# A gated-linear-attention mixer: decay factors from a running sum along the tokens, in place of matrix products with 0/1 masks

## The chip, the cores and the metric

The kernel runs on one core of a Trainium2 chip, in one launch. The metric is the device time of that launch in microseconds (us); lower is better. The engines are named as in the profile: PE multiplies matrices (PEld loads its weights), DVE does elementwise work on 128 lanes, ACT does elementwise functions and copies, POOL and SP here mostly issue transfers.

## The reference, cut to what matters

Two residual layers over 256 tokens of width 2048. Layer 0 mixes tokens with a gated recurrence (HGRN, eight heads) and an attention (FoX, eight heads); layer 1 mixes them with gated linear attention (GLA, four heads, key width 256, value width 512). Each layer ends with a feed-forward network. Float32 throughout. The part that the change touches is the GLA mixer:

```python
def gla_mixer(h, w_in, w_gate_up, b_gate, out_gain, w_out):
    q, k, v, g, g_low = jnp.split(h @ w_in, cuts, axis=-1)
    log_alpha = jax.nn.log_sigmoid(g_low @ w_gate_up + b_gate) / 16.0
    o = chunk_gated_linear_recurrence(split_heads(q, 4) * (256 ** -0.5), split_heads(k, 4),
                                      split_heads(v, 4), split_heads(log_alpha, 4))
    o = merge_heads(rms_norm(o, out_gain)) * jax.nn.silu(g)
    return o @ w_out
# recurrence: S_t = diag(exp(log_g_t)) S_{t-1} + k_t v_t^T ;  o_t = S_t^T q_t
# so score(t, s) = sum_d q[t,d] k[s,d] exp(cum[t,d] - cum[s,d]), cum = running sum of log_g, for s <= t
```

## The kernel before

**The stream.** Almost all the work is products of the 256-token activations with weights from memory, cut into *pieces* of 256 rows by 512 columns of weights. Each piece comes as float32 and is split in two: `hi`, a rounded copy made by ACT (line 166), and `lo`, the rest, made by DVE (line 168). PE then does 12 matmuls of 512 columns for it (lines 189 to 191: hi by hi, lo by hi, hi by lo; two token tiles of 128, two blocks of rows). `hi` and `lo` have four buffers each (`HIS = 4`), so the casts of piece n can start when PE has finished piece n - 4. Pieces are numbered through the program; the GLA mixer's products are pieces 392 to 487 (24 for each of four *units* C0 to C3, one for each head: part 0 gives q and k, part 1 v, part 2 the output gate), and the output projection O1 begins at piece 488.

**The recurrence of a unit** is woven between the pieces as a *job*: a list of steps to be issued within a number of pieces (`TICKS`). A scheduler then sets each engine's order from its own timeline model. For one GLA unit:

- `gla_gates`: z = low-rank gate input times `gate_up`, tokens on the partitions (line 824); log-sigmoid of z on ACT and DVE (lines 292 to 294, 827); split into a high and a low part, `lf` (lines 831 and 832).
- `Recurrence.transpose`: q and k turned so that channels lie on the partitions, `qkTs` (lines 433 to 436).
- `Recurrence.decays` (lines 448 to 456), for each token tile t and each half i of the head's channels: four matmuls `ex` of 512 columns multiply `lf` with the constant 0/1 matrix `lvl`, which sums the logs between two tokens for seven halving levels (64, 32, ... 1) and the tile's start or end; ACT takes exp of both halves from PSUM (line 455). The result `dec` has eight blocks of 128 columns.
- `Recurrence.factors`: DVE multiplies `dec` by the turned k into `kd` and by the turned q in place (line 465).
- `scores`, `cross`, `pick`, `output`: PE makes compact scores `sc` for each level (line 490), `cx` between the tiles (line 496); ACT and DVE scatter them into `st` (lines 514, 518); PE multiplies by v into `po` (lines 529 to 532).
- `gla_output`: norm, gate, turn back (`oT`, line 920), scale and split into `ct_m` (lines 375, 376), which is the operand of O1.

The layer-0 recurrence uses the same class with the same mask products.

Also on DVE, once in four pieces: the adaLN sums `mod` (line 108), a 2048-column product-and-sum.

Of the kernel before, what the change touches and what calls it, by code (L numbers as in the profile page):

```python
# [15 lines left out]
P = 128  # L16
# [13 lines left out]
# pieces of the products within which the mixers' steps are to be issued  # L30
# [9 lines left out]
# columns of the packed per-partition parameters  # L40
# [10 lines left out]
class Job:  # L51
    """Steps of arithmetic to be issued between the pieces of the streamed products, before a given piece."""
# [13 lines left out]
def build(tc, ctx, a, out):  # L66
# [212 lines left out]
    def rsqrt(dst, ss, n, width, name):  # L279
        """(ss / n + eps) ** -0.5 with one Newton step."""  # L280
# [50 lines left out]
    def norm_tile(t):  # L331
        """Normalize, modulate, transpose and split one token tile of x."""
# [47 lines left out]
    def gate_line(l, part):  # L380
        """The gate as a line in DRAM."""
# [35 lines left out]
    class Recurrence:  # L417
        """Both token tiles of one head. q, k: [P, tile, d]; lf: [P, tile, 2, d] (split); v: [P, tile, dv]."""

        def __init__(self, pool, q, k, lf, nd, name):  # L420
            self.pool, self.q, self.k, self.lf, self.nd, self.name = pool, q, k, lf, nd, name
            self.qkT, self.dec, self.kd, self.dg = {}, {}, {}, {}
            self.kc = {}
            self.s_t = st[Recurrence.count % 2]
            Recurrence.count += 1
# [31 lines left out]

        def factors(self, t, i):
# [8 lines left out]
            if t == 0:  # L467
# [6 lines left out]
                else:  # L474
                    self.kc[i] = kd[:, 0, :]
            else:
# [5 lines left out]
        def scores(self, t, levels, dst):  # L482
            """dst(n) -> PSUM [P, 64] of level n"""
            for n in levels:
                b = LEVELS[n]
                p = POS[t][b]
# [5 lines left out]
        def cross(self, diagonal):  # L492
            """Scores between the token tiles, and with diagonal those of each token with itself."""
            cx = ps_mix(f"cx_{self.name}")
            for i in range(self.nd):
                nc.tensor.matmul(cx[:, :P], self.kc[i], self.dec[1, i][:, 3, :], start=(i == 0), stop=(i == self.nd - 1))
# [10 lines left out]
        def pick(self, n, ts, src):  # L507
            """scatter the compact scores of level n; src: [P, len(ts), 64]"""
# [62 lines left out]
    def hgrn_scores(u, h):  # L571
# [3 lines left out]
        def s0():  # L575
            r = Recurrence(env["pool"], e["qg"][:, :, h * P:(h + 1) * P], e["k"][:, :, h * P:(h + 1) * P],
                           e["lf"][:, :, :, h * P:(h + 1) * P], 1, f"A{u}{h}")
# [64 lines left out]
    def fox_gates():  # L642
        """-log f, split, [token, head] per token tile; and -F in columns."""
# [157 lines left out]
    # =========================== layer 1 mixer ===========================  # L801
    def gla_low():
        """The low-rank gate input, transposed: 16 rows by w's high part, 16 by its low part, then ones for the bias."""
# [9 lines left out]
    def gla_gates(u):  # L813
        pool = env["pool"]
        f = pool.tile([P, 2, 2, 256], F32R, tag="lf", name=f"lf_C{u}", bufs=1)
        env.setdefault(("C", u), {})["lf"] = f
        c = {}

        def s0():
            gup = pool.tile([64, 256], F32, tag="gup", name=f"gup_{u}", bufs=1)  # L820
            nc.sync.dma_start(out=gup, in_=a["gate_up"][:, u * 256:(u + 1) * 256])
            z = ps_mix(f"z_C{u}").rearrange("p (t c) -> p t c", t=2)
            for t in range(2):
                nc.tensor.matmul(z[:, t], env["glT"][:, t * P:(t + 1) * P], gup, start=True, stop=True)
            sp = pool.tile([P, 2, 256], F32, tag="gt", name=f"sp_C{u}")
# [4 lines left out]
        def s1():  # L830
            nc.vector.tensor_scalar(f[:, :, 0], c["sp"], 1.0 / 16.0, None, ALU.mult)
            nc.vector.scalar_tensor_tensor(f[:, :, 1], c["sp"], 1.0 / 16.0, f[:, :, 0], ALU.mult, ALU.subtract)
# [18 lines left out]
    def gla_scores(u):  # L851
# [3 lines left out]
        def s0():  # L855
            r = Recurrence(env["pool"], e["qk"][:, :, :256], e["qk"][:, :, 256:], e["lf"], 2, f"C{u}")
            e["r"] = c["r"] = r
            if u < 2:
                nc.gpsimd.memset(r.s_t, 0.0)  # no diagonal of the HGRN units
# [4 lines left out]
        def tile_steps(t):  # L864
            def d0():
                c["r"].decays(t, 0)

            def d1():
                c["r"].decays(t, 1)
# [17 lines left out]
    def gla_output(u):  # L887
        """(steps that need v, steps that need the gate too)"""
# [217 lines left out]
    def begin_out(l, src):  # L1106
        """The old x and the gate row take buffers that the mixer's activations leave."""
# [97 lines left out]
    def begin_gla():  # L1205
        env["act"] = env["next_act"]
        open_pool("mix_b")

# [74 lines left out]
def _tiles(w, groups):  # L1283
    """w (K, N) and lists of 512 columns -> (chunk, quad, 128, 4 * 512)."""
# [70 lines left out]
```

## Time and profile before

| | us |
|---|---|
| median of three runs (lowest, highest) | 2520.81 (2519.14, 2520.96) |
| span of the profiled execution, first to last instruction | 2515.9 |
| around the span, median less span | 4.9 |
| PE busy in the span | 2450.4 (97%) |
| DVE busy | 1771.8 (70%) |
| ACT busy | 1160.2 (46%) |
| granted TensorE clock, mean share of full speed | 0.998 |

The three runs lie within 1.8 us. The GLA mixer takes the stretch from 1348 to 1681 us of the span. PE's busy time counts overlapping matmuls once, so 97% says that PE almost never stands still, not how well it is used.

### The profile page before, as it was taken

To read this page: it belongs to the slowest core of one execution; us is meant where nothing else is said; L and a number is where in the kernel's file an instruction comes from. 1 tells how busy PE (TensorE), PEld (TensorE's weight loads), DVE (VectorE), ACT (ScalarE), POOL (GpSimd) and SP (SyncE) were. 2 spreads that over 40 slices of the span, in tenths; PEclk is the share of its full clock that TensorE was granted. 3 is DMA by queue.
4 is the path that set the end of the run, shared out by engine and by line. 5 is a ranking of instruction groups with operands and counts; after the bars stand their busy time and mean duration, and the time that the engine had idled before them with its cause. 6 is when DMAs were issued, how large, how long until landed. Compare 5 with 4: busy or idle time off the path is not lost.

```text
span 2515.9 us, 28838 instructions
## 1 busy us (share of the span) xinstructions
PE 2450.4 (97%) x11316; PEld 2025.2 (80%) x11316; DVE 1771.8 (70%) x1975; ACT 1160.2 (46%) x1600; POOL 89.4 (4%) x174
## 2 busy tenths in 40 slices
PE   5899999999999999999999999999999999999999
PEld 3678887887888888888888888888788888888887
DVE  6986887877688767766777777777676545554555
ACT  4365555545434444344345545554544344344443
POOL 0000000000000000000000000000000000000000
PEclk9999999999999999999999999999999999999999
DMA  9973767885899878777776566677477555555554
GB/s 379 422 272 140 274 257 292 340 319 216 287 349 357 317 281 293 287 277 293 287 277 226 202 243 233 242 256 283 169 296 254 191 194 184 196 188 186 199 185 149
DMA packets 93850, 647.49 MB, mean 257 GB/s; under 512 B 10417, under 2 KB 10993, under 8 KB 16401
## 3 DMA queue, kind: packets, MB, share of 16 engines
q1 hardware_dynamic: 70290, 476.59, 52.1%
q0 software_dynamic: 23424, 169.07, 18.1%
q8 instruction: 88, 1.44, 0.2%
q14 instruction: 48, 0.39, 0.0%
HBM read 641.39 MB, written 4.23 MB: 257 GB/s over the span
## 4 chain that ended last, share of the span: by engine, by line
PE 92%; DVE 6%; ACT 1%; issue 0%; DMA 0%; SPq 0%; ACTq 0%; DVEq 0%
PE acc_F L191 13%; PE acc_F L190 13%; PE acc_F L189 13%; PE acc_G L189 6%; PE acc_G L191 6%; PE acc_G L190 6%; PE acc_C L191 4%; PE acc_C L189 4%; PE acc_C L190 3%; DVE mod_s L108 3%; PE acc_B L189 2%; PE acc_B L190 2%; PE acc_B L191 2%; PE acc_O L189 2%; PE acc_O L191 2%; PE acc_O L190 2%
## 5 line engine op out<-in xcount | busy, mean ns | idle before, releaser
L168 DVE TENSOR_TENSOR lo<-raw_F,hi 128x1024 fp32r<-128x1024 f32 x352 | 429.4, 1224 | 296.9 <-ACT hi L166 296.8
L166 ACT CAST hi<-raw_F 128x1024 fp32r<-128x1024 f32 x352 | 370.5, 1053 | 478.3 <-PE acc_F L191 430.0
L191 PE MATMUL acc_F<-hi,hT_f 128*128 128x512 f32 x1408 | 551.3, 392 | 1.4 <-DVE hT_f L355 1.4
L189 PE MATMUL acc_F<-hi,hT_f 128*128 128x512 f32 x1408 | 548.4, 390 | 1.8 <-ACT hT_f L354 1.8
L190 PE MATMUL acc_F<-lo,hT_f 128*128 128x512 f32 x1408 | 548.5, 390 | 0.0
L108 DVE SCALAR_TENSOR_TENSOR mod<-mod,silu_c 128x2048 f32<-128x2048 f32 x160 | 365.4, 2285 | 11.1 <-DMA mod<-in_mod_w_dram 11.1
L168 DVE TENSOR_TENSOR lo<-raw_G,hi 128x1024 fp32r<-128x1024 f32 x176 | 214.2, 1222 | 138.3 <-ACT hi L166 138.1
L191 PEld LDWEIGHTS acc_F<-hi,hT_f 128*128 128x128 f32 x1408 | 264.4, 188 | 56.6 <-DVE hT_f L355 3.0
L189 PEld LDWEIGHTS acc_F<-hi,hT_f 128*128 128x128 f32 x1408 | 264.5, 188 | 56.1 <-ACT hT_f L354 2.2
L166 ACT CAST hi<-raw_G 128x1024 fp32r<-128x1024 f32 x176 | 185.4, 1054 | 268.6 <-PE acc_G L191 224.8
L190 PEld LDWEIGHTS acc_F<-lo,hT_f 128*128 128x128 f32 x1408 | 264.3, 188 | 55.2
L189 PE MATMUL acc_G<-hi,ct_f 128*128 128x512 f32 x704 | 273.5, 389 | 1.6 <-DVE res_G L403 1.6
L191 PE MATMUL acc_G<-hi,ct_f 128*128 128x512 f32 x704 | 274.4, 390 | 0.0
L190 PE MATMUL acc_G<-lo,ct_f 128*128 128x512 f32 x704 | 273.8, 389 | 0.0
L168 DVE TENSOR_TENSOR lo<-raw_C,hi 128x1024 fp32r<-128x1024 f32 x96 | 116.8, 1222 | 58.4 <-ACT hi L166 58.0
L189 PEld LDWEIGHTS acc_G<-hi,ct_f 128*128 128x128 f32 x704 | 132.2, 188 | 29.6 <-DVE res_G L403 2.4
L189 PE MATMUL acc_C<-hi,hT_n 128*128 128x512 f32 x384 | 154.3, 402 | 0.9 <-ACT hT_n L354 0.9
L190 PEld LDWEIGHTS acc_G<-lo,ct_f 128*128 128x128 f32 x704 | 132.2, 188 | 27.4
L191 PEld LDWEIGHTS acc_G<-hi,ct_f 128*128 128x128 f32 x704 | 132.2, 188 | 27.2
L191 PE MATMUL acc_C<-hi,hT_n 128*128 128x512 f32 x384 | 150.5, 392 | 0.7 <-DVE hT_n L355 0.7
L190 PE MATMUL acc_C<-lo,hT_n 128*128 128x512 f32 x384 | 150.9, 393 | 0.0
L166 ACT CAST hi<-raw_C 128x1024 fp32r<-128x1024 f32 x96 | 100.7, 1052 | 94.7 <-PE acc_C L191 88.4
(335 smaller groups left out, 3424.0 us busy)
## 6 DMA issues: line engine op xcount, KB each, us to landing
raw_F<-in_ffn_w_in_dram SPq DMA_DIRECT2D x176, 1024.0 KB, 4.9
mod<-in_mod_w_dram POOLq DMA_DIRECT2D x160, 1024.0 KB, 5.2
raw_G<-in_ffn_w_out_dram SPq DMA_DIRECT2D x88, 1024.0 KB, 4.9
raw_C<-in_gla_w_in_dram SPq DMA_DIRECT2D x48, 1024.0 KB, 6.0
mod_s<-in_mod_w_dram SPq DMA_DIRECT2D x32, 1024.0 KB, 10.6
raw_B<-in_ab_w_in_dram SPq DMA_DIRECT2D x32, 1024.0 KB, 5.9
raw_s<-in_start_w_dram SPq DMA_DIRECT2D x16, 1024.0 KB, 8.8
raw_A<-in_ab_w_in_dram SPq DMA_DIRECT2D x16, 1024.0 KB, 5.0
```

What stands on the lines that cost most here:

```text
L108: nc.vector.scalar_tensor_tensor(tile, tile, 1.0, silu_c, ALU.mult, ALU.mult, accum_out=modc[l, part][:, j:j + 1])
L166: nc.scalar.copy(out=hi, in_=w)
L168: env["lo"] = nc.vector.tensor_tensor(lo, w, hi, ALU.subtract)
L189: nc.tensor.matmul(o, a_hi, w_hi, start=(kt == 0), stop=False)
L190: nc.tensor.matmul(o, a_hi, w_lo, start=False, stop=False)
L191: nc.tensor.matmul(o, a_lo, w_hi, start=False, stop=(kt == last))
```

## The change

Only GLA's decays change; layer 0's recurrence keeps the mask products.

- The gate product is turned: `gate_up` columns are the weights, the gate input the moving side, so that z and its log-sigmoid `sp` have channels on the partitions and tokens along the row. The count and size of the matmuls stay.
- Instead of the split into `lf`, two scans (one for each half of the channels, 256 tokens) make `cum`, the running sum of `sp`. A constant `reset` (1, and 0 at each tile's first token; two memsets on POOL) makes the sum start anew in each token tile.
- `decays_of_sums` replaces `decays`: for each tile and half, six DVE subtractions of 128 columns (levels 32 to 1) give cum less its value at each block's middle; four ACT operations take absolute values and then exp(-x/16): two of 128 columns with a bias read from `cum` (the tile block and level 64), one of 768 columns, one of 1024 columns for the exp.
- `factors` for the second tile makes one product of 768 columns for `kd` instead of two of 384.
- Block positions are the same for both tiles, so `scores` and `cross` read other blocks of the same sizes.

The other lines of the diff remove comments.

```diff
+        def decays_of_sums(self, t, i):
+            dec = self.pool.tile([P, 8, P], F32, tag="dec", ...)
+            c = self.cum[i][:, t * P:(t + 1) * P]
+            for b in LEVELS[1:]:
+                src = c.rearrange("p (n w) -> p n w", w=2 * b)
+                nc.vector.tensor_tensor(dec[:, POS[0][b], :].rearrange("p (n w) -> p n w", w=2 * b), src,
+                                        src[:, :, b - 1:b].to_broadcast([P, 64 // b, 2 * b]), ALU.subtract)
+            if t == 0:
+                nc.scalar.activation(dec[:, 0, :], c, AF.Abs, scale=-1.0, bias=c[:, P - 1:P])
+            else:
+                nc.scalar.activation(dec[:, 0, :], c, AF.Abs)
+            nc.scalar.activation(dec[:, 1, :], c, AF.Abs, scale=-1.0, bias=c[:, 63:64])
+            nc.scalar.activation(dec[:, 2:, :], dec[:, 2:, :], AF.Abs)
+            nc.scalar.activation(dec, dec, AF.Exp, scale=-self.scale)
+            self.dec[t, i] = dec
...
+            elif self.cum is not None:
+                mul(kd, 1, 7, kT)
+                mul(dec, 0, 8, qT)
...
-            for t in range(2):
-                nc.tensor.matmul(z[:, t], env["glT"][:, t * P:(t + 1) * P], gup, start=True, stop=True)
+            for i in range(2):
+                nc.tensor.matmul(z[:, i], gup[:, i * P:(i + 1) * P], env["glT"], start=True, stop=True)
...
-            nc.vector.tensor_scalar(f[:, :, 0], c["sp"], 1.0 / 16.0, None, ALU.mult)
-            nc.vector.scalar_tensor_tensor(f[:, :, 1], c["sp"], 1.0 / 16.0, f[:, :, 0], ALU.mult, ALU.subtract)
+            for i in range(2):
+                nc.vector.tensor_tensor_scan(cum[:, i], env["reset"], c["sp"][:, i], 0.0, ALU.mult, ALU.add)
...
-                c["r"].decays(t, 0)
+                c["r"].decays_of_sums(t, 0)
...
+        reset = env["reset"] = env["pool"].tile([P, 2 * P], F32, tag="reset", name="reset", bufs=1)
+        nc.gpsimd.memset(reset, 1.0)
+        nc.gpsimd.memset(reset.rearrange("p (t c) -> p t c", t=2)[:, :, 0:1], 0.0)
```

Since the scheduler sets the order, each engine's queue changes in the GLA stretch and at the start of O1; outside these nothing moves. Three places follow. In the names, the first number after `hi_`, `lo_` is the piece.

PE in unit C2, around piece 457, before: matmuls `ex` stand between those of the pieces.

```order
L191 MATMUL acc_C22_11693<-hi_456_11634,hT_n1_0_9854 128x512
L454 MATMUL ex_C2_1_1_0_11710<-lvl_75,lf_C2_11449 128x512 x2
L189 MATMUL acc_C22_11693<-hi_457_11660,hT_n1_0_9854 128x512
L190 MATMUL acc_C22_11693<-lo_457_11661,hT_n1_0_9854 128x512
L191 MATMUL acc_C22_11693<-hi_457_11660,hT_n1_0_9854 128x512
L189 MATMUL acc_C22_11693<-hi_457_11660,hT_n1_0_9854 128x512
L454 MATMUL ex_C2_1_1_1_11714<-lvl_75,lf_C2_11449 128x512 x2
L190 MATMUL acc_C22_11693<-lo_457_11661,hT_n1_0_9854 128x512
```

The same place after:

```order
L191 MATMUL acc_C22_11714<-hi_456_11653,hT_n1_0_9854 128x512
L189 MATMUL acc_C22_11714<-hi_457_11679,hT_n1_0_9854 128x512
L190 MATMUL acc_C22_11714<-lo_457_11680,hT_n1_0_9854 128x512
L191 MATMUL acc_C22_11714<-hi_457_11679,hT_n1_0_9854 128x512
L189 MATMUL acc_C22_11714<-hi_457_11679,hT_n1_0_9854 128x512
L190 MATMUL acc_C22_11714<-lo_457_11680,hT_n1_0_9854 128x512
```

The pieces follow each other without `ex`; all 16 such matmuls of each unit are gone.

DVE in unit C1, from the log-sigmoid to `lo` of piece 431, before:

```order
L827 SCALAR_TENSOR_TENSOR sp_C1_10836<-z_C1_10833,sp_C1_10836 128x512
L831 TENSOR_SCALAR lf_C1_10830<-sp_C1_10836 128x2x256
L168 TENSOR_TENSOR lo_428_10903<-raw_C11_2_10760,hi_428_10902 128x1024
L832 SCALAR_TENSOR_TENSOR lf_C1_10830<-sp_C1_10836,lf_C1_10830 128x2x256
L168 TENSOR_TENSOR lo_429_10930<-raw_C11_2_10760,hi_429_10929 128x1024
L168 TENSOR_TENSOR lo_430_10960<-raw_C11_3_10797,hi_430_10959 128x1024
L108 SCALAR_TENSOR_TENSOR mod1_3_15_10977,modc1_3_91<-mod1_3_15_10977,silu_c_72 128x2048
L465 TENSOR_TENSOR kd_C1_0_0_10954<-dec_C1_0_0_10920,qkTs_C1_0_10887 128x896
L168 TENSOR_TENSOR lo_431_10987<-raw_C11_3_10797,hi_431_10986 128x1024
```

And after (a scan is printed as SCALAR_TENSOR_TENSOR, line 856). Ahead of this, DVE now also has the last steps of unit C0 (`ct_m`), of which two rows show.

```order
L851 SCALAR_TENSOR_TENSOR sp_C1_10845<-z_C1_10842,sp_C1_10845 128x512
L376 SCALAR_TENSOR_TENSOR ct_m1_0_10701<-oT_C00_10696,cols_73,ct_m1_0_10701 128x256
L856 SCALAR_TENSOR_TENSOR cum_C1_10839<-reset_10036,sp_C1_10845 128x256 x2
L168 TENSOR_TENSOR lo_428_10912<-raw_C11_2_10769,hi_428_10911 128x1024
L467 TENSOR_TENSOR dec_C1_0_0_10929<-cum_C1_10839 128x128 x3
L376 SCALAR_TENSOR_TENSOR ct_m1_0_10701<-oT_C01_10722,cols_73,ct_m1_0_10701 128x256
L467 TENSOR_TENSOR dec_C1_0_0_10929<-cum_C1_10839 128x128 x3
L467 TENSOR_TENSOR dec_C1_0_1_10956<-cum_C1_10839 128x128 x6
L168 TENSOR_TENSOR lo_429_10941<-raw_C11_2_10769,hi_429_10940 128x1024
L485 TENSOR_TENSOR kd_C1_0_0_10967<-dec_C1_0_0_10929,qkTs_C1_0_10896 128x896
L168 TENSOR_TENSOR lo_430_10973<-raw_C11_3_10806,hi_430_10972 128x1024
L108 SCALAR_TENSOR_TENSOR mod1_3_15_10990,modc1_3_91<-mod1_3_15_10990,silu_c_72 128x2048
```

After these come the q product of `dec` (896 columns) and `lo` of piece 431. Twelve subtractions and two scans have come in between the `lo` casts, and the steps behind them stand later against the pieces: `oT` of unit C2 stood within piece 466 on PE before, and stands within piece 469 now.

PE at the start of O1 after. O1's first column block needs `ct_m1_3`, the last unit's result, from piece 494 on. Before, PE did 494, 495, 496 in this order; after:

```order
L191 MATMUL acc_O1_0_12566<-hi_493_12643,ct_m1_2_11949 128x512
L189 MATMUL acc_O1_1_12744<-hi_496_12697,ct_m1_0_10701 128x512
L189 MATMUL acc_O1_0_12566<-hi_494_12659,ct_m1_3_12587 128x512
L190 MATMUL acc_O1_0_12566<-lo_494_12660,ct_m1_3_12587 128x512
L190 MATMUL acc_O1_1_12744<-lo_496_12698,ct_m1_0_10701 128x512
L191 MATMUL acc_O1_1_12744<-hi_496_12697,ct_m1_0_10701 128x512
```

Pieces 496 and 497 of the second column block now stand ahead of most of 494; 495 and 498 follow them.

## Rows read from the trace of the kernel before

**Rows 1.** The page: span, busy time by engine, the ending chain.

```profile
span 2515.9 us, 28838 instructions
...
PE 2450.4 (97%) x11316; PEld 2025.2 (80%) x11316; DVE 1771.8 (70%) x1975; ACT 1160.2 (46%) x1600; POOL 89.4 (4%) x174
...
PE 92%; DVE 6%; ACT 1%; issue 0%; DMA 0%; SPq 0%; ACTq 0%; DVEq 0%
```

**Rows 2.** Busy by stretch: us; PE, PEld, DVE, ACT, POOL (instructions); clock, DMA, GB/s.

```profile
1446.00:1510.00 64.00, 64.00 (x317) 53.17 (x317) 48.82 (x63) 31.45 (x48) 2.64 (x5) 1.00 0.68 245
...
1348.00:1681.00 333.00, 332.31 (x1611) 273.77 (x1611) 241.94 (x319) 174.26 (x269) 11.62 (x22) 1.00 0.64 231
```

**Rows 3.** PE's groups, 1348 to 1690 us: busy us, mean ns | idle before.

```profile
L454 PE MATMUL ex_C<-lvl,lf_C 128*128 128x512 f32 x64 | 19.0, 398 | 0.0
```

**Rows 4.** PE in order of time, unit C0: start us, us of all, count.

```profile
1398.20 1.10 PE L454 MATMUL ex_C<-lvl,lf_C 128*128 128x512 f32 x4
1399.13 0.40 PE L191 MATMUL acc_C<-hi,hT_n 128*128 128x512 f32 x1
```

**Rows 5.** DVE's groups, same stretch and columns as rows 3.

```profile
L168 DVE TENSOR_TENSOR lo<-raw_C,hi 128x1024 fp32r<-128x1024 f32 x92 | 112.1, 1222 | 58.4 <-ACT hi L166 58.0
L108 DVE SCALAR_TENSOR_TENSOR mod<-mod,silu_c 128x2048 f32<-128x2048 f32 x23 | 52.5, 2285 | 0.0
...
L465 DVE TENSOR_TENSOR kd_C<-dec_C,qkTs_C 128x896 f32<-128x896 f32 x8 | 8.6, 1085 | 0.0
...
L465 DVE TENSOR_TENSOR kd_C<-dec_C,qkTs_C 128x384 f32<-128x384 f32 x16 | 8.3, 552 | 3.0 <-ACT dec_C L455 3.0
...
L376 DVE SCALAR_TENSOR_TENSOR ct_m<-oT_C,cols,ct_m 128x256 fp32r<-128x256 f32 x12 | 5.2, 478 | 1.6 <-ACT ct_m L375 1.6
...
L444 DVE SCALAR_TENSOR_TENSOR dgj_C<-qk_C 128x256 f32<-128x256 f32 x8 | 3.1, 420 | 0.0
...
L832 DVE SCALAR_TENSOR_TENSOR lf_C<-sp_C,lf_C 128x512 fp32r<-128x512 f32 x4 | 2.7, 684 | 0.0
...
L831 DVE TENSOR_SCALAR lf_C<-sp_C 128x512 fp32r<-128x512 f32 x4 | 1.7, 428 | 0.1
```

**Rows 6.** DVE in order of time, 1400 to 1417 us, unit C0.

```profile
1400.17 2.09 DVE L465 TENSOR_TENSOR kd_C<-dec_C,qkTs_C 128x896 f32<-128x896 f32 x2
...
1412.69 0.22 DVE L518 COPY_PREDICATED st<-lmask,sc_C 128x64 f32<-128x64 int32 x1
...
1416.66 0.62 DVE L518 COPY_PREDICATED st<-lmask,sc_C 128x64 f32<-128x64 int32 x2
```

**Rows 7.** ACT's groups, same stretch and columns as rows 3.

```profile
L166 ACT CAST hi<-raw_C 128x1024 fp32r<-128x1024 f32 x92 | 96.5, 1052 | 93.9 <-PE acc_C L191 88.4 <-issue 4.6 <-ACT hi L166 0.8
L455 ACT ACTIVATE dec_C<-ex_C 128x512 f32<-128x512 f32 x32 | 17.6, 595 | 8.7 <-PE ex_C L454 5.2 <-PE sc_C L490 3.4
...
L293 ACT ACTIVATE sp_C<-sp_C 128x512 f32<-128x512 f32 x4 | 2.5, 634 | 0.1
...
L472 ACT COPY kc_C<-kd_C 128x128 f32<-128x128 f32 x8 | 2.3, 293 | 0.3 <-DVE kd_C L465 0.3
```

**Rows 8.** All engines in order of time, gate product to log-sigmoid, unit C0.

```profile
1384.95 1.13 PE L824 MATMUL z_C<-gup,glT 64*128 64x256 f32 x4
...
1386.01 0.50 PE L191 MATMUL acc_C<-hi,hT_n 128*128 128x512 f32 x1
...
1388.08 0.69 DVE L827 SCALAR_TENSOR_TENSOR sp_C<-z_C,sp_C 128x512 f32<-128x512 f32 x1 [1.84 <-ACT sp_C L294]
```

**Rows 9.** ACT in order of time in O1: casts one piece apart; `ct_m` casts.

```profile
1692.63 0.83 ACT L375 ACTIVATE ct_m<-oT_C,cols 128x256 fp32r<-128x256 f32 x2
...
1697.19 1.06 ACT L166 CAST hi<-raw_O 128x1024 fp32r<-128x1024 f32 x1 [1.66 <-PE acc_O L191]
1699.92 1.05 ACT L166 CAST hi<-raw_O 128x1024 fp32r<-128x1024 f32 x1 [1.68 <-PE acc_O L191]
```

More of the change, by code (lines that the diff above doesn't have):

```diff
@@ L417, in build, with __init__ @@
     class Recurrence:
-        def __init__(self, pool, q, k, lf, nd, name):
+        def __init__(self, pool, q, k, nd, name, lf=None, cum=None, scale=1.0):
             self.pool, self.q, self.k, self.lf, self.nd, self.name = pool, q, k, lf, nd, name
+            self.cum, self.scale = cum, scale
+            self.pos = POS if cum is None else (POS[0], POS[0])
             self.qkT, self.dec, self.kd, self.dg = {}, {}, {}, {}
@@ L456, in decays @@
             self.dec[t, i] = dec
+        def decays_of_sums(self, t, i):
+            dec = self.pool.tile([P, 8, P], F32, tag="dec", name=f"dec_{self.name}_{t}_{i}")
+            c = self.cum[i][:, t * P:(t + 1) * P]
[11 more added lines that the diff above has]
+            self.dec[t, i] = dec
         def factors(self, t, i):
@@ L485, in scores @@
                 b = LEVELS[n]
-                p = POS[t][b]
+                p = self.pos[t][b]
                 for i in range(self.nd):
@@ L494, in cross @@
             cx = ps_mix(f"cx_{self.name}")
+            p = 3 if self.cum is None else 0
             for i in range(self.nd):
-                nc.tensor.matmul(cx[:, :P], self.kc[i], self.dec[1, i][:, 3, :], start=(i == 0), stop=(i == self.nd - 1))
+                nc.tensor.matmul(cx[:, :P], self.kc[i], self.dec[1, i][:, p, :], start=(i == 0), stop=(i == self.nd - 1))
             if diagonal:
@@ L576, in s0 @@
             r = Recurrence(env["pool"], e["qg"][:, :, h * P:(h + 1) * P], e["k"][:, :, h * P:(h + 1) * P],
-                           e["lf"][:, :, :, h * P:(h + 1) * P], 1, f"A{u}{h}")
+                           1, f"A{u}{h}", lf=e["lf"][:, :, :, h * P:(h + 1) * P])
             e["r", h] = c["r"] = r
@@ L814, in gla_gates @@
         pool = env["pool"]
-        f = pool.tile([P, 2, 2, 256], F32R, tag="lf", name=f"lf_C{u}", bufs=1)
-        env.setdefault(("C", u), {})["lf"] = f
+        cum = pool.tile([P, 2, T], F32, tag="lf", name=f"cum_C{u}", bufs=1)
+        env.setdefault(("C", u), {})["cum"] = cum
         c = {}
@@ L821, in s0 @@
             nc.sync.dma_start(out=gup, in_=a["gate_up"][:, u * 256:(u + 1) * 256])
-            z = ps_mix(f"z_C{u}").rearrange("p (t c) -> p t c", t=2)
-            for t in range(2):
-                nc.tensor.matmul(z[:, t], env["glT"][:, t * P:(t + 1) * P], gup, start=True, stop=True)
-            sp = pool.tile([P, 2, 256], F32, tag="gt", name=f"sp_C{u}")
+            z = ps_mix(f"z_C{u}").rearrange("p (i t) -> p i t", i=2)
+            for i in range(2):
+                nc.tensor.matmul(z[:, i], gup[:, i * P:(i + 1) * P], env["glT"], start=True, stop=True)
+            sp = pool.tile([P, 2, T], F32, tag="gt", name=f"sp_C{u}")
             softplus_neg_abs(sp, z)
@@ L855, in s0 @@
         def s0():
-            r = Recurrence(env["pool"], e["qk"][:, :, :256], e["qk"][:, :, 256:], e["lf"], 2, f"C{u}")
+            r = Recurrence(env["pool"], e["qk"][:, :, :256], e["qk"][:, :, 256:], 2, f"C{u}",
+                           cum=[e["cum"][:, i] for i in range(2)], scale=1.0 / 16.0)
             e["r"] = c["r"] = r
@@ L865, in d0 @@
             def d0():
-                c["r"].decays(t, 0)
+                c["r"].decays_of_sums(t, 0)
             def d1():
-                c["r"].decays(t, 1)
+                c["r"].decays_of_sums(t, 1)
                 c["r"].factors(t, 0)
```

## The prediction

> **What bounds the kernel now.** I read the page first: PE is busy in 97% of the span, DVE in 70%, ACT in 46%, and the chain of work that ended last runs through PE for 92%, with no share for transfers [rows 1]. The DVE share of that chain, 6%, belongs to the adaLN sums of the start. Then the stretch that the change touches: in the GLA mixer PE is busy in 332.31 of 333 us and in all 64 us of the stretch inside it, at full clock [rows 2]. So here the end moves by what leaves PE, as long as nothing makes PE wait. Third, what keeps the weights coming: ACT's `hi` casts wait 88.4 of their 93.9 idle us for PE to free a buffer, and DVE's `lo` casts wait for `hi` [rows 5, 7]. The casts thus run as early as the four buffers allow. A cast of one piece follows that of the last after 2.73 us [rows 9], PE's pace. `lo` of piece n is there 1.05 + 1.22 = 2.3 us after PE ends piece n - 4 [rows 5, 7] and is used 3 x 2.73 = 8.2 us after it: a **lead of 5.9 us**. DVE and ACT may fall behind by that much before PE stands.
>
> **What leaves PE.** Each unit has 2 tiles x 2 halves x 4 = 16 mask matmuls `ex`, 64 in four units [rows 3]. Four of them take from 1398.20 to the next matmul's start at 1399.13 us, 0.93 us, so 0.2325 each [rows 4]; PE did not idle before any [rows 3]. 64 x 0.2325 = **14.9 us** go. The turned gate product keeps its four matmuls' count and size, and the scores keep theirs: nothing. The mean duration of `ex` is 398 ns [rows 3], but each overlaps its neighbours, so that product (25.5 us) is not the price. The Trainium skill, Perfetto Trace Analysis, section Identifying the Most-Contended Engine, says the same, that matmul busy time is a bad measure because matmuls are pipelined; who takes durations forecasts 10.6 us more than I do.
>
> **What DVE gains.** From the `kd` products, (1085 - 552) / (896 - 384) = 1.04 ns a column and 152 ns fixed; two back to back take 2.09 instead of 2.17 us, so about 80 ns of that is hidden in a row of instructions [rows 5, 6]. A subtraction of 128 columns is then 0.205 us in a row and 0.285 alone. For the levels 2 and 1, whose runs are four and two columns long, the nearest rows are the predicated copies: 0.22 us with long runs, 0.62 for two with the shortest, so 0.09 more for 64 columns and up to 0.17 for 128 [rows 6]. Twelve subtractions (one tile) are between 12 x 0.205 = 2.5 and 12 x 0.285 + 4 x 0.17 = 4.1 us. I take 12 x 0.285 = 3.4, the isolated price, since waits fall between. The trace has no scan. The bounds are an operation on the same 256 columns, 0.42, and one on 512, 0.68 [rows 5]; I take 0.42 as the nearer shape and keep the other. The skill's page DVE: opcode table, instruction layouts, handler registers and perf-mode slots, section Datapath and trigger behaviour, says that the scan runs at half throughput; no run here shows it yet. By it the upper bound is the price, and a unit's sum grows by 0.5 us of DVE time that PE doesn't see.
>
> Per unit: 2 x 3.4 + 2 x 0.42, less `lf` (0.43 + 0.68), less twice the saving of one 768-column product for two of 384 (2 x 0.55 - 0.95 = 0.15) [rows 5]: +6.2 us, at the upper bounds +8.2. DVE had 241.94 / 4 = 60.5 us of 83.3 per unit [rows 2]; now 66.7 of 79.5 (84%).
>
> **What ACT gains.** Eight exps of 0.595 go, 4.8 us per unit [rows 7]. From the 512- and 128-column rows (634 and 293 ns) a column costs 0.89 ns; a tile and half now needs 2 x 0.29 + 0.86 + 1.09 = 2.5 us, a unit 10.1. Net +5.4, to 49 of 79.5 us. POOL's two memsets lie beside everything, as POOL works 11.6 of 333 us [rows 2]. No queue of SP is moved past anything but by a piece or two.
>
> **Does a burst reach PE?** Totals fit; what matters is the queue. The added work comes in eight bursts (two tiles, four units), and a `lo` cast behind it is late if DVE is. I follow the one that looks tightest, unit C1's first tile, up to `lo` of piece 431. Let 0 be PE's start on `z`. PE: 1.06 us for z [rows 8], then seven pieces of 2.73, so 431 starts at 20.2 and first needs `lo` 0.2 later (transposes in between, not counted, make it later still). DVE: before, sp began 3.1 us after z [rows 8]; now two casts of C0's `ct_m` (0.83) [rows 9] and one `hi` (1.05) [rows 7] stand ahead on ACT: 5.0. From there DVE has, by its order, sp 0.69 (like `lf`'s 512 columns) [rows 5], two `ct_m` 0.96, scans 0.84, `lo` of 428 to 431 4.89, twelve subtractions 3.4, two products 2.17, one adaLN sum 2.29 [rows 5]: 15.2, less 80 ns for each of some twelve rows in a row, 14.2. It ends at 19.2: **1.2 us to spare**. The upper bounds add 0.7 + 0.5 = 1.2 and use it up exactly. The q products come later and carry only scores, which have slack of pieces in the new order. For the second tiles I find the same size of margin, since there PE also has the scores in between. I put **0.3 us** of waiting into the sum for all eight, bounds 0 and 4 (half a microsecond in each, if ACT's chain adds to the upper prices).
>
> **The start of O1.** The unit's steps end about three pieces later than before, so `ct_m1_3` is only just made when O1 wants it. Let E be the end of piece 493. The last casts of `ct_m1_3` stand behind `hi` and `lo` of 497, which wait for the buffer of 493: ACT is done at E + 1.05 + 0.42, DVE at E + 1.05 + 1.22 + 0.48 = E + 2.75 [rows 5, 7, 9]. In the old order the ninth matmul of 494 would want the latter at E + 1.8 and stand 1.0 us. In the new one, 496 and half of 497 go first and it is wanted at about E + 4.4: no wait. But 494 is then finished only at E + 8.2; `hi` and `lo` of 498 come at E + 10.5 against a use at E + 10.9, 499 at E + 13.2 against E + 13.6. Margins of 0.4. I take **0.3**, bounds 0 and 1.0.
>
> **Sum.** -14.9 + 0.3 + 0.3 = -14.3 us. The profiled execution's span of 2515.9 becomes 2501.6; the median lies 4.9 above the span, and the O1 and feed-forward stages behind are bound by PE, so they carry the shift to the end: 2520.8 - 14.3 = **2506.5 us**. What is late next is PE again.
>
> **Rivals.**
> 1. *Bursts that reach PE.* If the fine-grained subtractions or the chain scan, absolute value, exp, products cost more than any row here, each burst runs past its margin. At 1 us in each of eight, 8 us of the 14.9 come back: 2513.9. For it: the margin is only 1.2 us by estimate, and in the new PE order pieces 431, 455 and 479 are cut after one matmul for the next piece's first, as if `lo` were expected late. Against: I used isolated prices.
> 2. *Slower: DVE sets the pace of the mixer.* Same place. The 14.9 us are lost if each burst passes its margin by 1.9, that is, costs 3.1 us more: it decides at 0.285 + 3.1 / 12 = 0.54 us a subtraction. At 0.7 each burst costs 3.8 beyond the margin, 30 us in all: 2536. No row of 128 or fewer columns is near that (0.31 the worst) [rows 6].
> 3. *The change gains nothing, as transfers take PE's place.* Weights come at 231 GB/s with DMA engines 0.64 busy [rows 2] and would need 4% more. Against: the chain has no DMA. About 2520.
>
> **How the numbers follow.** Forecast (own range 2504.8 to 2509): 0.72. Rival 1: 0.18, of which I count a fifth within the band. Rival 2: 0.04. Rival 3 and losses of its size: 0.06. Within 0.2%, about what a measurement of this kernel can tell from no change, is 5.0 us: faster means below 2515.8. Faster 0.72 + 0.14 = 0.86, same 0.04 + 0.06 less a little that goes past = 0.09, slower 0.05. The range reaches from 2504.5 (all waits nil, and 1 us for the spread of runs) into rival 1, to 2512: that leaves out some 0.1 above 2512 from rival 1's upper part and some 0.1 from rivals 2 and 3.
>
> **What would show it.** After: no `ex` group on PE; 11252 matmuls; PE busy still about all of the mixer, which ends some 14 us earlier; DVE about 267 of 319 us. Right if PE shows next to no idle time that a `lo` ended, with subtractions of 0.2 to 0.3 us. Rival 1 shows as waits of PE on line 168 at pieces 431, 455, 479 and in the second tiles; rival 2 as such waits all over. The forecast is wrong if scans cost a microsecond or more, or if O1 waits long on `ct_m`.

## The result and the profile after

The changed kernel takes 2505.03 us in the median (2501.8 to 2505.51) against 2519.97 us (2517.94 to 2520.96) of the kernel before on the same chip: ratio 0.9936, 95% interval 0.9922 to 0.995. A second comparison, with more runs, gave 2505.21 us (2503.61 to 2507.83) against 2519.57: ratio 0.9948, 0.9935 to 0.996. Both intervals hold 0.994, that is 15 us less. The forecast was 2506.5, with a range from 2504.5 to 2512.

The page of the changed kernel, beside [rows 1]: the span, busy time and instructions by engine, and the chain that ended last.

```profile
span 2503.7 us, 28790 instructions
...
PE 2438.0 (97%) x11252; PEld 2014.8 (80%) x11252; DVE 1788.5 (71%) x2063; ACT 1178.3 (47%) x1632; POOL 89.9 (4%) x176
...
PE 92%; DVE 6%; ACT 1%; issue 0%; DMA 0%; SPq 0%; ACTq 0%; DVEq 0%
```

PE lost exactly the 64 matmuls (11316 to 11252); DVE gained 16.7 us of work (25 by forecast), ACT 18.1 (22), and the chain still runs through PE.

The GLA mixer by stretch, beside [rows 2] (us; busy time of PE, PEld, DVE, ACT, POOL; granted clock; DMA share; GB/s):

```profile
1351.00:1668.00 317.00, 316.31 (x1548) 261.87 (x1547) 260.33 (x403) 192.24 (x297) 12.51 (x25) 1.00 0.68 244
```

DVE is now busy for 82% of the mixer (before: 73%; 84% by forecast), and PE still for all of it but 0.7 us. All waits of PE between 1340 and 1760 us, by what it waited for (us in total, times, longest):

```profile
PE acc_C L189 <- ACT hT_n L354: 0.9, 1, 0.9
PE acc_G L189 <- DVE res_G L403: 0.8, 1, 0.8
PE acc_O L189 <- DVE res_O L403: 0.8, 1, 0.8
PE acc_C L191 <- DVE hT_n L355: 0.7, 1, 0.7
```

Two stand at the norm ahead of the mixer (`hT_n`) and two at residual additions, that of the feed-forward network before it and that of O1 (`res`); the change touches neither. No `lo`, no score and no `ct_m` is among them: **both waiting terms of the sum were nil**.

The groups of DVE and ACT in the mixer (busy us, mean ns of one | idle before), beside [rows 5, 7]:

```profile
L168 DVE TENSOR_TENSOR lo<-raw_C,hi 128x1024 fp32r<-128x1024 f32 x92 | 111.4, 1220 | 35.0 <-ACT hi L166 34.7
L166 ACT CAST hi<-raw_C 128x1024 fp32r<-128x1024 f32 x92 | 96.4, 1050 | 63.3 <-PE acc_C L191 56.7 <-issue 5.2 <-ACT cs_C L526 0.7
L467 DVE TENSOR_TENSOR dec_C<-cum_C 128x128 f32<-128x128 f32 x96 | 20.1, 284 | 4.1 <-PE sc_C L513 4.1
...
L475 ACT ACTIVATE dec_C<-dec_C 128x1024 f32<-128x1024 f32 x16 | 16.7, 1051 | 0.0
...
L474 ACT ACTIVATE dec_C<-dec_C 128x768 f32<-128x768 f32 x16 | 13.0, 841 | 0.6 <-DVE dec_C L467 0.6
L473 ACT ACTIVATE dec_C<-cum_C 128x128 f32<-128x128 f32 x16 | 6.2, 389 | 0.0
L856 DVE TENSOR_TENSOR_SCAN cum_C<-reset,sp_C 128x256 f32<-128x256 f32 x8 | 5.1, 678 | 0.2
L470 ACT ACTIVATE dec_C<-cum_C 128x128 f32<-128x128 f32 x8 | 3.2, 397 | 0.6 <-DVE cum_C L856 0.5
```

The casts show where the slack went: the idle time of `lo` ahead of its casts fell from 58.4 to 35.0 us and that of `hi` from 93.9 to 63.3, while PE lost nothing. The change spends the lead of the casts. How much is left is seen in the unit that the prediction followed, C1's first tile. DVE there (start us, us of all, count):

```profile
1463.00 0.69 DVE L851 SCALAR_TENSOR_TENSOR sp_C<-z_C,sp_C 128x512 f32<-128x512 f32 x1 [0.41 <-ACT sp_C L294]
...
1464.00 1.26 DVE L856 TENSOR_TENSOR_SCAN cum_C<-reset,sp_C 128x256 f32<-128x256 f32 x2
...
1467.30 1.89 DVE L467 TENSOR_TENSOR dec_C<-cum_C 128x128 f32<-128x128 f32 x9
...
1475.69 1.22 DVE L168 TENSOR_TENSOR lo<-raw_C,hi 128x1024 fp32r<-128x1024 f32 x1
```

and PE, with the gate product and the first matmul that reads this last `lo`, that of piece 431:

```profile
1458.95 1.13 PE L848 MATMUL z_C<-glT,gup 64*128 64x256 f32 x4
...
1480.73 0.48 PE L190 MATMUL acc_C<-lo,hT_n 128*128 128x512 f32 x1
```

From PE's start on `z`, `lo` is ready after 1476.91 - 1458.95 = 18.0 us and is used after 21.8: 3.8 us early, where the forecast had 19.2 and 20.4, 1.2 early. The same reckoning for every piece of the mixer, from the records of both engines, puts the tightest at 455 and 479 (2.8 us) and 407 (2.9); in the kernel before the least was 3.3 (both without the first few pieces behind the norm, which are alike). The tightest of all is the start of O1: `lo` of piece 496 is 1.2 us early. It is ready at 1685.63 + 1.22 = 1686.85, and the second of the two matmuls in the PE row, 0.23 us behind the first, reads it:

```profile
1685.63 1.22 DVE L168 TENSOR_TENSOR lo<-raw_O,hi 128x1024 fp32r<-128x1024 f32 x1
1687.83 0.62 PE L190 MATMUL acc_O<-lo,ct_m 128*128 128x512 f32 x2
```

### The profile page after: what moved, and what is told of

It reads as the page before. It is cut to its first block, busy times and chain, and to the rows that moved or that the text cites. A ratio compares the mean times of both kernels' runs of the same rounds, so it can differ in the third digit from the quotient of the medians.

```text
span 2503.7 us, 28790 instructions
## 1 busy us (share of the span) xinstructions
PE 2438.0 (97%) x11252; PEld 2014.8 (80%) x11252; DVE 1788.5 (71%) x2063; ACT 1178.3 (47%) x1632; POOL 89.9 (4%) x176
## 4 chain that ended last, share of the span: by engine, by line
PE 92%; DVE 6%; ACT 1%; issue 0%; DMA 0%; SPq 0%; ACTq 0%; DVEq 0%
PE acc_F L191 13%; PE acc_F L189 13%; PE acc_F L190 13%; PE acc_G L189 6%; PE acc_G L190 6%; PE acc_G L191 6%; PE acc_C L191 4%; PE acc_C L189 4%; PE acc_C L190 4%; DVE mod_s L108 3%; PE acc_B L189 2%; PE acc_B L190 2%; PE acc_B L191 2%; PE acc_O L189 2%; PE acc_O L190 2%; PE acc_O L191 2%
## 5 line engine op out<-in xcount | busy, mean ns | idle before, releaser
L108 DVE SCALAR_TENSOR_TENSOR mod<-mod,silu_c 128x2048 f32<-128x2048 f32 x160 | 365.3, 2284 | 10.3 <-DMA mod<-in_mod_w_dram 10.3
L103 POOL DMA_DIRECT2D mod<-in_mod_w_dram x160 | 84.7, 529 | 1613.2 <-DVE mod L108 1451.4
```

The source lines that it names most:

```text
L103: nc.gpsimd.dma_start(out=tile, in_=a["mod_w"][l, part * KT + j])
L108: nc.vector.scalar_tensor_tensor(tile, tile, 1.0, silu_c, ALU.mult, ALU.mult, accum_out=modc[l, part][:, j:j + 1])
```

## The experiments

Theory A: in the GLA mixer PE's pitch is the time; the 64 matmuls are worth 0.2325 us each, and what DVE and ACT got stays inside the lead of the casts. Its rivals: the matmuls are worth more (their durations); other parts of the change gain or cost; the bursts reach PE.

**The changed kernel again**, in more rounds, no edit.

> The changed kernel itself, in five rounds against the kernel before, to settle the size. Theory A (only the 64 mask matmuls count, at their pitch of 0.2325 us, or 15.0 us as the mixer's own length in the two traces says): 14.9 to 15.1 us less, ratio 0.9940. The recorded forecast (14.9 less 0.6 of waits): 14.3 less, 0.9943. Rival B (each matmul counts nearly its own duration of 398 ns): 25 less, 0.990. Rival C (something outside the mixer gained too, as the first comparison's 0.9936 may say): 16 or more less, 0.9936 or below.

Ratio 0.9948 (0.9935 to 0.996). Rival B (0.990) falls. Rival C's 0.9936 lies just inside the interval, so the times alone don't exclude it, and they can't tell 0.9940 from 0.9943. The traces can: the mixer and O1, from the first matmul of the one to the last of the other, are the stretch in which the change can act. It became 14.9 us shorter (below), and the span as a whole only 12.2 (2515.9 to 2503.7), so nothing outside it gained.

**Half of the matmuls away, nothing added.** The kernel before, GLA's masks on the high part alone:

```
-                for w in range(2):
-                    nc.tensor.matmul(ps, self.lf[:, t, w, ...], ..., start=(w == 0), stop=(w == 1))
+                n = 1 if self.nd > 1 else 2
+                for w in range(n):
+                    nc.tensor.matmul(ps, self.lf[:, t, w, ...], ..., start=(w == 0), stop=(w == n - 1))
```

> The kernel before, with one edit: in the GLA mixer the mask matmuls take the high part of the log decays only (the low part is made but not used, so the decays are a little less exact). 32 of the 64 matmuls go; DVE and ACT do what they did. Theory A (PE's pitch is the price): 32 x 0.2325 = 7.4 us less, ratio 0.9970. Rival B (duration is the price): 12.7 less, 0.9950. Rival D (the gain came from the other parts of the change, not from these matmuls): no change, 1.000.

2511.63 us against 2519.57, ratio 0.9969 (0.9958 to 0.9979): A's 0.9970. Rival B's 0.9950 is outside the interval, and so is D's 1.000.

**The matmuls put back** into the changed kernel:

```
+            for part in range(2):
+                ps = ps_mix(...)
+                for w in range(2):
+                    nc.tensor.matmul(ps, lvl[:, w * P:(w + 1) * P], lvl[:, c0:c0 + 512], ...)
+                nc.scalar.copy(out=env["sink"], in_=ps[:, 0:1])
```

> The changed kernel with PE's removed work put back: in each of the 16 steps four 512-column matmuls of constants, whose results nobody needs but for one column that ACT copies to a scratch tile, so that the PSUM buffer is held as before. DVE keeps the subtractions and scans, ACT the absolute values. Theory A: the time before comes back, 64 x 0.2325 = 14.9 more than the changed kernel, ratio 0.999 to 1.001 against the kernel before. Rival D (the other parts gain or cost by themselves): below 0.998 or above 1.002.

2519.43 us against 2519.57, ratio 0.9999 (0.999 to 1.0008): with PE's work back, the time of before is back, although DVE and ACT do all the new work. So the gain is PE's matmuls, and the new work costs nothing that these runs can tell (the interval reaches from 2.5 us below to 2.0 above).

The lengths say the same. For each kernel the matmuls of the mixer and of the output products (count; duration min/median/max; first and last start in us): before,

```profile
L189 PE MATMUL acc_C<-hi,hT_n x384: 387/389/799, 1347.8 to 1681.7; 128*128 128x512 f32 x192
...
L191 PE MATMUL acc_O<-hi,ct_m x256: 387/389/482, 503.7 to 1771.2; 128*128 128x512 f32 x128
```

changed,

```profile
L189 PE MATMUL acc_C<-hi,hT_n x384: 387/389/799, 1350.5 to 1667.6; 128*128 128x512 f32 x192
...
L191 PE MATMUL acc_O<-hi,ct_m x256: 387/389/628, 503.3 to 1759.0; 128*128 128x512 f32 x128
```

and with the matmuls put back,

```profile
L189 PE MATMUL acc_C<-hi,hT_n x384: 387/389/798, 1349.5 to 1683.4; 128*128 128x512 f32 x192
...
L191 PE MATMUL acc_O<-hi,ct_m x256: 387/389/628, 502.2 to 1772.9; 128*128 128x512 f32 x128
```

From the mixer's first start to O1's last: 423.4, 408.5 and 423.4 us. The change is worth **14.9 us** there, 64 x 0.233. The start of the mixer itself wanders between 1347.8 and 1350.5 in these executions, ahead of everything that differs. With half the matmuls away,

```profile
L189 PE MATMUL acc_C<-hi,hT_n x384: 387/389/799, 1349.0 to 1677.2; 128*128 128x512 f32 x192
...
L191 PE MATMUL acc_O<-hi,ct_m x256: 387/389/482, 502.2 to 1766.7; 128*128 128x512 f32 x128
```

it is 417.7, and in the second execution of the changed kernel 410.0, but these two had a granted clock of 0.88 in the first 14 us around the mixer's start, which costs 0.12 x 14 = 1.7: without it 416.0 and 408.3, 7.4 and 15.1 less than before. That stretch in the two executions of the changed kernel, the first and the second:

```profile
1347.00:1361.00 14.00, 12.41 (x82) 10.73 (x80) 11.17 (x27) 8.45 (x22) 0.00 (x0) 1.00 0.50 169
```

```profile
1347.00:1361.00 14.00, 12.41 (x63) 10.00 (x62) 9.49 (x25) 8.64 (x22) 0.00 (x0) 0.88 0.39 132
```

The same program, with the same idle time, has the full clock there once and loses 1.7 us of it the other time.

**How much more would DVE bear?** The changed kernel with each subtraction done two, three or four times:

```
-                nc.vector.tensor_tensor(dec[...], src, src[...].to_broadcast(...), ALU.subtract)
+                for _ in range(2):   # 3, 4
+                    nc.vector.tensor_tensor(dec[...], src, src[...].to_broadcast(...), ALU.subtract)
```

> The changed kernel with every subtraction of the prefix sums done twice into the same tile: each burst of twelve costs DVE 12 x 0.205 = 2.5 us more. Theory A (the tightest lo casts of the mixer were 2.8 us early in the changed kernel's trace, at the pieces 407, 455 and 479): nothing reaches PE, the time stays that of the changed kernel, ratio 0.9943 against the kernel before. Rival 1 as recorded (1.2 us to spare at 431, so 1.3 us a burst get through): 8 x 1.3 = 10 us more, 0.998.

> The same with every subtraction done three times, 0.615 us for one, 5.0 us more a burst. By the forecast's working for rival 2 the gain is lost from 0.54 us on, so this one would be slower than the kernel before: 8 x (12 x 0.615 - 3.4 - 1.2) = 22 us more than the changed kernel, ratio 1.003. Theory A (margins of 2.8 at three or four bursts, 4 to 6 at the others): 4 x 2.2 and at most 4 x 1, 5 to 13 us more, 0.996 to 0.9995.

> The same with every subtraction done four times, 0.82 us for one, 7.5 us more a burst. Theory A: every burst now passes its margin, by 4.7 us at the tight ones and 2 to 3 at the others, 28 us more than the changed kernel, ratio 1.005. By the forecast's margin of 1.2 us: 8 x (12 x 0.82 - 3.4 - 1.2) = 42 us more, 1.011. If PE's waits also lower its granted clock, as in the kernel with both mixers turned, more than that.

Ratios 0.9948 (0.9933 to 0.9963), 1.0034 (1.0021 to 1.0047) and 1.0128 (1.0111 to 1.0145). With twice the subtractions the ratio is that of the changed kernel, and rival 1's 0.998 is outside the interval; but the interval is wide enough (3.8 us either way) to hide a few us. The trace shows them:

```profile
L189 PE MATMUL acc_C<-hi,hT_n x384: 387/389/799, 1348.2 to 1658.4; 128*128 128x512 f32 x192
...
L191 PE MATMUL acc_O<-hi,ct_m x256: 387/389/499, 504.0 to 1761.2; 128*128 128x512 f32 x128
```

From the mixer's first start to O1's last are 413.0 us, 4.5 more than in the changed kernel, of which 2.3 are a wait of PE for a `lo` at O1's start (row below), 0.6 one for `ct_m`, and 1.6 stay open. So theory A's "nothing reaches PE" holds for the bursts in the mixer and not for O1. Three times loses the whole gain: 9.0 us above the kernel before, where the changed kernel was 14.4 below it, so 23 us, what the forecast's working for rival 2 gives (22) and not theory A's 5 to 13. Four times costs 46, by the forecast's working 42, by A 28. But the place is another one than both had in mind. With three times the subtractions, PE's longest waits from 1690 us on are these:

```profile
PE sc_C L514 <- DVE dec_C L486: 9.3, 2, 9.1
PE oT_C L946 <- DVE o_C L938: 3.9, 2, 3.6
```

and two stretches of the same kernel, the mixer's last third and the middle of O1, read (columns as above):

```profile
1540.00:1640.00 100.00, 100.00 (x472) 81.83 (x471) 88.83 (x159) 54.78 (x78) 4.22 (x8) 1.00 0.69 255
1690.00:1740.00 50.00, 36.17 (x166) 27.86 (x165) 35.19 (x77) 17.52 (x34) 1.06 (x2) 0.86 0.29 100
```

In this stretch of the mixer PE is busy all the time, at 89% DVE load and with no wait for a `lo`. In this kernel the steps of the last unit stand later in PE's order, so that its scores come when O1 has only products left that need that unit's result. Then the chain of subtractions, exp and products stands open: PE is idle for 13.8 of 50 us, and its granted clock there averages 0.86 of full speed, since it was at 1.2 GHz for parts of the stretch, which costs up to 7 more. From the mixer's first start to O1's last this kernel takes 433.2 us, 24.7 more than the changed kernel; its new waits, the first of them at 1676 us, on O1's `lo`, add up to 16.3 us, and the lower clock behind 1640 us costs up to 8.5. Together they cover the difference. With the subtractions doubled, the first wait to appear is also at O1's start:

```profile
PE acc_O L190 <- DVE lo L168: 2.3, 1, 2.3
```

So the margin that gave out first was that of O1 (1.2 us), not those of the eight bursts. These three kernels also shift the scores against the pieces by themselves, so they say where the slack ends, not what a slower subtraction would cost in the order of the changed kernel.

**The first mixer too.** The changed kernel with the first mixer's decays turned by PE transposes and scanned as well:

```
-            nc.vector.tensor_scalar(f[:, :, 0], l0, LOG_MIN_FORGET, None, ALU.max)
-            nc.vector.scalar_tensor_tensor(f[:, :, 1], l0, LOG_MIN_FORGET, f[:, :, 0], ALU.max, ALU.subtract)
+            nc.vector.tensor_scalar(l0, l0, LOG_MIN_FORGET, None, ALU.max)
+            for h in range(2):
+                for t in range(2):
+                    nc.tensor.transpose(lT[:, h, t * P:(t + 1) * P], l0[:, t, h * P:(h + 1) * P], ident)
+            for h in range(2):
+                nc.vector.tensor_tensor_scan(cum[:, h], env["reset"], lT[:, h], 0.0, ALU.mult, ALU.add)
...
-            c["r"].decays(0, 0)
+            c["r"].decays_of_sums(0, 0)
```

> The changed kernel, with the first mixer's recurrence turned as well: its log decays, clamped in token-major form as before, are turned by four PE transposes a unit, scanned from PSUM, and its 64 mask matmuls go. Theory A (PE sets the pace there too): 64 x 0.2325 = 14.9 less and 16 transposes of 0.11 = 1.8 more, 13.1 less than the changed kernel, ratio 0.9888 against the kernel before. Rival E (DVE is too full in the first mixer: busy 107 of 135 and 115 of 140 us in two stretches of it, and a unit's 24 subtractions of 0.205, two scans of 0.68, less 0.7 for the low part, add 5.6 us): the bursts reach PE, and half or more of it comes back, ratio 0.991 to 0.994.

2529.84 us, ratio 1.0045 (1.0033 to 1.0058): 24.6 us **slower** than the changed kernel with 64 matmuls less, beyond what rival E allowed. PE's waits in the first layer's mixer, 190 to 620 us, of this kernel, the longest three:

```profile
PE sc_A L513 <- DVE dec_A L485: 11.4, 2, 6.7
PE acc_B L189 <- DVE g_B L797: 7.7, 2, 3.9
PE po_A L556 <- DVE st L546: 6.4, 2, 3.3
```

In the changed kernel the first is absent, the second 4.3 and the third 1.1 us. And three stretches of that mixer, first of the changed kernel, then of this one:

```profile
200.00:270.00 70.00, 67.68 (x360) 57.79 (x359) 47.92 (x74) 36.47 (x71) 1.82 (x3) 0.98 0.49 177
330.00:400.00 70.00, 64.96 (x345) 55.48 (x346) 58.11 (x83) 38.10 (x95) 5.37 (x11) 0.97 0.72 265
400.00:470.00 70.00, 70.00 (x343) 58.76 (x342) 57.18 (x78) 41.20 (x101) 5.80 (x11) 0.98 0.83 315
```

```profile
200.00:270.00 70.00, 60.39 (x312) 52.76 (x312) 53.95 (x115) 46.49 (x88) 1.06 (x2) 0.85 0.37 132
330.00:400.00 70.00, 58.62 (x289) 49.15 (x288) 53.41 (x96) 38.55 (x86) 4.77 (x9) 0.88 0.64 240
400.00:470.00 70.00, 60.51 (x280) 51.33 (x279) 50.88 (x77) 35.03 (x103) 4.86 (x10) 0.88 0.63 235
```

`g_B` is the gate of the attention, which DVE makes from the accumulator `acc_B`; PE's next product waits until that accumulator is free. PE is idle some 23 us more in the three, and the clock column falls from 0.97-0.98 to 0.85-0.88: up to (0.13 + 0.09 + 0.10) x 70 = 22 us at full speed are lost to the clock in addition, less what falls into the waits. That eats the 13 us of matmuls and more. DVE is no busier than before (158 against 163 us in the three), so it isn't full: what is late is one head's chain. The explanation that the next run tests: its two decay tiles fill both buffers, so the next head's subtractions stand behind the scores that free them, while PE has only scores next. These rows show the wait, not yet its cause.

**Four buffers for the decay tiles**, to let the subtractions run ahead (to make room, the mask constants go and the scan's ones and zeros take two bytes each):

```
-            dec = self.pool.tile([P, 8, P], F32, tag="dec", ...)
+            dec = self.pool.tile([P, 8, P], F32, tag="dec", bufs=env.get("decs", 2), ...)   # 4 in the first mixer
```

> Both mixers by prefix scan, as before, but in the first mixer the decay tiles have four buffers instead of two, for which the mask constants, now without use, make room (and the zeros and ones of the scan are stored in 2 bytes). Theory F (in the run with two buffers the subtractions of a head stood behind the scores of the head before it, and PE, which had only scores next, waited 6.7 us for them): the subtractions run ahead, PE's waits on dec go, and with them the half clock that followed: 13 us less than the changed kernel, ratio 0.989. Rival E (DVE is too full whatever the buffers): as slow as with two, 1.003 to 1.006.

2514.65 us, ratio 0.9975 (0.9965 to 0.9986). Against the medians of before in its own comparison it is 6.2 us below, where the run with two buffers was 10.3 above and the changed kernel 14.4 below: 16 of the 25 us come back, which fits the explanation, though the scheduler's order changed with the buffers and the two were not separated; 8 are still lost. The wait for `dec` falls to 3.3 us, but another grows:

```profile
PE acc_B L188 <- DVE g_B L786: 10.5, 2, 6.7
PE sc_A L502 <- DVE dec_A L474: 3.3, 1, 3.3
```

**Subtractions on POOL** in the first mixer, on top of that:

```
-                nc.vector.tensor_tensor(dec[...], ..., ALU.subtract)
+                (nc.gpsimd if self.nd == 1 else nc.vector).tensor_tensor(dec[...], ..., ALU.subtract)
```

> Both mixers by prefix scan with four decay buffers, and in the first mixer the subtractions run on the idle POOL instead of DVE. Theory G (DVE's 4.9 us a unit of subtractions were what made PE wait): ratio below 0.9975, towards 0.989. Rival H (it is the length of a head's chain, from its scan to its products, and not DVE's load): POOL's subtractions, if slower than DVE's 0.205 us, lengthen it, and PE waits more than with DVE, above 0.9975.

2528.24 us, ratio 1.0032 (1.002 to 1.0044), as rival H had it. POOL takes 617 ns for what DVE does in 0.21 us in a row:

```profile
L456 POOL TENSOR_TENSOR dec_A<-cum_A 128x128 f32<-128x128 f32 x96 | 56.1, 617 | 40.2 <-PE sc_A L502 33.5 <-issue 4.7 <-DVE cum_A L581 1.6
```

But PE's wait for `dec` stays at 3.2 us; what grew is the wait for `g_B`, from 10.5 to 17.6:

```profile
PE acc_B L188 <- DVE g_B L786: 17.6, 2, 13.8
```

That the longer chain of a head makes the attention's gate late is likely, but no run shows it.

**Only less work in the first mixer.** The changed kernel with the first mixer's masks on the high part alone, and the low part not made:

```
-                for w in range(2):
-                    nc.tensor.matmul(ps, self.lf[:, t, w, ...], ..., start=(w == 0), stop=(w == 1))
+                nc.tensor.matmul(ps, self.lf[:, t, 0, ...], ..., start=True, stop=True)
...
-            nc.vector.scalar_tensor_tensor(f[:, :, 1], l0, LOG_MIN_FORGET, f[:, :, 0], ALU.max, ALU.subtract)
```

> The changed kernel, and in the first mixer the mask matmuls take the high part of the log decays only; its low part is not made (those decays are a little less exact). 32 matmuls go there, DVE loses one 512-column operation a unit. Theory A (PE sets the pace there too, and nothing is added on another engine): 32 x 0.2325 = 7.4 us less than the changed kernel, ratio 0.991 against the kernel before. Rival E (the first mixer is held by DVE, so that PE's lighter load turns into waits): no change from the changed kernel, 0.9943.

2515.32 us against 2521.26, ratio 0.9978 (0.997 to 0.9987): 5.9 below the kernel before and so 8 us slower than the changed kernel, although no engine has more to do. Neither theory had that. PE's two longest waits in that mixer, and one of the three stretches:

```profile
PE acc_B L189 <- DVE g_B L790: 8.3, 2, 4.5
PE sc_A L512 <- DVE dec_A L484: 5.1, 1, 5.1
```

```profile
400.00:470.00 70.00, 65.20 (x308) 54.94 (x308) 49.80 (x76) 40.00 (x111) 5.37 (x11) 0.89 0.63 237
```

With other costs the order of the steps came out different (scores and transposes of the first units stand at other pieces), and in this order PE waits and loses clock. Whether the new order or the missing cover of the matmuls does it was not separated: every kernel that takes matmuls out of the first mixer also got another order. What the four runs show together is that, in each of these edits, matmuls taken out of the first mixer did not come back as time, as they do in the second.

## Why the prediction was right in its mechanism and wrong in its waits

**The step that failed.** The first term of the sum held. The two waiting terms did not: 0.3 us for the bursts and 0.3 for the start of O1 were forecast, and PE waited 0 us at either. The margins that led to them were too slim, 1.2 us where 3.8 were measured at piece 431: the subtractions were priced as if each stood alone (3.4 us a tile against 2.5), and the transposes ahead of this piece on PE were named and not counted. The rest of the distance is the base, a median of 2520.81 us from three runs where the comparison gave 2519.97. Of the 1.5 us between 2506.5 and 2505.03 the waits are 0.6 and the base 0.8: 2519.97 - 14.9 = 2505.1. That this meets the median so closely is luck, as the medians of the kernel before differ by up to 1.7 us between comparisons.

**What leaves PE.** 64 x 0.2325 = 14.9: measured 14.9 between the mixer's first and O1's last start, the same with half of the matmuls (7.4 for 32), and zero when they were put back. The pitch, not the 398 ns of [rows 3], was the price. The Trainium skill, Perfetto Trace Analysis, section Identifying the Most-Contended Engine, calls matmul busy time a poor measure of how close a kernel is to its roofline, as matmuls are pipelined; as a price the durations misled here too (25.5 us by them, 14.9 measured). One reading was wrong without weight in the sum: of DVE's 6% in the ending chain of [rows 1] the profile gives the adaLN sums of the start 3%, not all.

**What DVE gains.** I took 0.285 us a subtraction, bounds 0.205 and above. Nine in a row took 1.89 us, 0.2 each and one hidden part on top: the lower bound, and levels with runs of two or four columns pay nothing extra, against the predicated copies of [rows 6]. I took 0.42 for a scan, bounds up to 0.68. It took 678 ns, two in 1.26 us: the upper bound. The Trainium skill, DVE: opcode table, instruction layouts, handler registers and perf-mode slots, section Datapath and trigger behaviour, has the scan at half throughput; the trace agrees, 678 ns for 256 columns beside 684 for a plain operation on 512 [rows 5]. Both choices were wrong and partly cancel: per tile 2.5 instead of 3.4 for the subtractions, per unit 1.26 instead of 0.84 for the scans.

**What ACT gains.** Absolute values with a bias took 389 and 397 ns, not 290; 768 and 1024 columns took 841 and 1051 ns as worked out (0.86 and 1.09). It cost nothing that the runs can tell, as ACT had room.

**Bursts.** The margin at piece 431 was 1.2 by forecast and 3.8 measured; the bursts' 0.3 us of waiting were 0. Of the 2.6 between them DVE gave 1.2: the log-sigmoid began 4.05 us after `z` and not 5.0, the subtractions took 0.9 less and the scans 0.4 more, with small waits between. PE gave 1.4: eight transposes, a matmul of 432 and a score stand ahead of this `lo`; I had named the transposes and not counted them.

**O1.** Margins of 0.4 by forecast, at 498 and 499; 1.2 the tightest measured, at 496, which the forecast didn't price; the 0.3 us were 0. That the place was tight is right: doubling the subtractions made PE wait first there.

**Rivals.** Rival 1 did not happen; rival 2's deciding point, 0.54 us a subtraction, lies between 0.41 (a loss of a few us at most) and 0.615 (slower than before), but its place was wrong: O1's start instead of every burst. That its 22 us for three times the subtractions met the measured 23 is luck. Rival 3 did not happen: 244 GB/s were reached in the mixer with no wait for a transfer.

**The base.** The forecast put the span's shift on a median 4.9 us above it. In the profiled execution of the changed kernel the time is 1.75 us more than the span (2505.45 against 2503.7). If that holds for the kernel before, its profiled execution took some 2517.7 us, an estimate, and was a quick one; the rest of the 4.9 was spread between executions. One source of the spread shows in the traces: short stretches at 1.2 GHz come in other numbers and places in each execution of the same kernel (at 553 and 611 us in one of the changed kernel, at 1350 in the other), and cost one to two us each. Medians of before came out at 2519.6 to 2521.3, single runs between 2516.0 and 2524.8. The 1 us for the spread at the range's lower edge was too little: the median of 2505.03 lies 0.5 above that edge, and one of its four runs, 2501.8, is below it. (By its own terms, 2520.8 - 14.9 - 1, the edge would be 2504.9 and not 2504.5.)

## What to carry to other kernels

Where one engine is busy for a whole stage, price what leaves it by the pitch in order of time, and price what its neighbours get by the lead that they have: here the tightest lead of a cast in the mixer fell from 3.3 to 2.8 us and the time didn't notice. Then look at the stage's end, where no further work covers a late chain: that is where the doubled load first showed and the tripled load lost 23 us. And an edit that pays in one stage need not pay in a similar one: in the first mixer the same edit cost 25 us, as PE there came to wait for a head's chain, and the stretches with these waits had more time at 1.2 GHz.

## What was new about the hardware

- Subtractions of 128 columns with a broadcast operand follow each other on DVE about 0.2 us apart (12 in 2.51), whatever the length of the runs; on POOL one takes 0.617 us.
- A prefix scan of 256 columns in f32 takes 678 ns, two in a row 1.26 us, about the time of a plain operation on twice the columns (684 ns for 512).
- An absolute value of 128 columns takes ACT 389 to 397 ns with a bias per partition and 311 without; a plain copy of them takes 293 ns [rows 7].
- Waits of PE come with a lower granted clock in the stretch: 0.85 to 0.88 in three stretches of 70 us with 9.5 to 11.4 us of idle time each, against 0.97 to 0.98 with 0 to 5 us of idle time in the kernel without these waits. In O1 the clock took up to half as much as the idle time (7 of 13.8), in the first mixer up to about as much (22 of 23).
